# The MLP norm's sums spread by a product with a matrix of ones

## The chip, the cores and the metric

The kernel runs on one core of a Trainium2 chip. The time is the device time of one execution in microseconds (us), and the number that counts is the median over several executions. Three executions of the kernel before took 1001.45, 1001.76 and 1002.26 us.

A core has five engines that run side by side, each with its own queue of instructions worked off in order: PE (TensorE, matrix products; PEld are its loads of the stationary operand), DVE (VectorE, elementwise), ACT (ScalarE, elementwise with a function), POOL (GpSimd) and SP (SyncE, which here only issues transfers). Products land in PSUM, in banks of 128 partitions by 512 fp32 numbers. DVE and ACT read PSUM and SBUF.

## The reference, cut to what matters

One layer of a hybrid decoder for 576 tokens (512 prompt tokens and 8 x 8 sample tokens), width 1024, hidden width of the MLP 4096. The part that matters here is the last:

```python
def rmsnorm(x, g, eps):
    xf = x.astype(jnp.float32)
    y = xf * lax.rsqrt(jnp.mean(xf * xf, axis=-1, keepdims=True) + eps)
    return (y * g.astype(jnp.float32)).astype(x.dtype)

x = x + m @ lp['w_out']
hn = rmsnorm(x, lp['g_ffn'], NORM_EPS)
x = x + jnp.square(jax.nn.relu(hn @ lp['w_up'])) @ lp['w_down']
...
y_prompt = rmsnorm(hp, g_final, NORM_EPS)
```

The MLP is quadratic in `hn`, so a factor that is the same for all features of a token can be pulled out of it: with M2 = mean(x²) + eps of a token, the MLP's result is that of the unscaled input divided by M2. The kernel uses this: it multiplies x by M2 before the down projection adds to it, and multiplies the sum by R2 = 1/M2 at the end.

## The kernel before, in words

Activations lie transposed: features on the 128 partitions (8 groups `d` of 128), the 576 tokens along the free axis, cut into two halves of 288 (`HALF = ((0, 288), (288, 288))`). A per-token factor such as M2 must therefore stand in every partition: `M2` and `R2` are tiles of 128 x 576 whose rows are all alike.

Every weight matrix arrives as fp32 and is split into a high and a low part of a shorter format (ACT writes the high part, DVE the rest), and each product is made of three: high·high, high·low, low·high. One such product of 128 x 128 with 288 columns is the unit of PE's work.

The stages of the end: output projection (tiles `ps_wo`), which writes x into `ya` (lines 1128 to 1167) and adds up the squares of x over the eight feature groups into `acc` (128 x 576: what is left is a sum over the 128 partitions); then the up projection in 16 pairs (`up_pair`, line 1180), each of seven block products of twelve matmuls by a Strassen-like scheme (PSUM tiles `ua`, `ub`, `uc`, `ud`, `ux`), whose results are squared and split into `q`; then the down projection (`down`, line 1266; PSUM tile `ps_dn`), whose results are added to `ya`. The loop at line 1280 runs eight chunks `ch` of two pairs; from chunk 1 on each pair is followed by four of the eight groups of the chunk before's down projection. The down projection of the last chunks (line 1304 on) multiplies by R2 and makes the final norm.

The norm of the MLP stands inside this loop, behind the first pair (lines 1283 to 1298). `colsum` (line 234) sums `acc` over the partitions with five products, each with 128 tokens of `acc` as the stationary operand and a column of ones as the moving one; the sums come out with tokens on the partitions, in a PSUM tile of 128 x 5. DVE makes the mean plus eps (`m2`, 128 x 5) and its reciprocal (`r2`). `spread` (line 245) brings each back into 128 equal rows: five transposes on PE of a column broadcast along the free axis, each into a PSUM bank of its own (`pb_M2`, `pb_R2`), each copied to SBUF by ACT. In the profile the numbers at the ends of names are left out, so the tiles appear as `pst`, `m`, `r`, `pb_M`, `pb_R`, `M`, `R`. Two other tiles of such names (of earlier norms) share rows with `pst` and `R`.

The order of the work on each engine is made ahead of time by a planner. It takes, among the instructions whose inputs and buffers it counts as ready, the one with the lowest priority number. `prio(...)` sets that number: `FEED + 1000 * job` (negative) for loads, splits and evictions that belong to product number `job`, `FILL + 1000 * job` (positive) for the matmuls themselves. `ring["job"]` counts the products. A small offset on it puts an instruction behind or ahead of others of the same job. The planner may take an instruction long before its place in the program, if it is ready. `bank(...)` takes one of three PSUM banks in rotation; the up pair's `ux` (line 1239) is from the same three. The multiplication of `ya` by `M2` has line 1273, in `down` for the chunk 0; in the profile it has the helper's line, L61.

Of the kernel before, what the change touches and what calls it, by code (L numbers as in the profile page):

```python
# [8 lines left out]
F32 = mybir.dt.float32  # L9
# [6 lines left out]
P = 128  # L16
D = 1024
# [11 lines left out]
HALF = ((0, 288), (288, 288))  # L29
# [12 lines left out]
def tile_hybrid_step(ctx, tc, xT, xsT, ktab, vtab, s0T, ptab, w_in, vecs, w2a2, g2, lamv,  # L42
# [3 lines left out]
    PE, VE, AE, GE = nc.tensor, nc.vector, nc.scalar, nc.gpsimd  # L46
    PS = bass.MemoryType.PSUM

    def pool(name, bufs=1, stack=ctx, **kw):
        return stack.enter_context(tc.tile_pool(name=name, bufs=bufs, **kw))  # L50
# [4 lines left out]
    ring = {"job": 0}  # L55

    def act(out, in_, func=AF.Copy, **kw):
        ring["act"] = AE.activation(out=out, in_=in_, func=func, **kw)  # L58
# [9 lines left out]
    def ts(out, a, s1, op0, s2=None, op1=ALU.bypass, eng=None):  # L68
        (eng or VE).tensor_scalar(out=out, in0=a, scalar1=s1, scalar2=s2, op0=op0, op1=op1)

    def mm(out, lhsT, rhs, start=True, stop=True):
        ring["mm"] = PE.matmul(out=out, lhsT=lhsT, rhs=rhs, start=start, stop=stop)  # L72
        return ring["mm"]

    def tr(out, in_, idn):
        ring["mm"] = PE.transpose(out=out, in_=in_, identity=idn)

    def bc(ap, shape):
        return ap.broadcast_to(shape)
# [3 lines left out]
    FEED, LATE, FILL = -1000000, 500000, 1000000  # L83

    @contextmanager
    def prio(at):
        was, tc.cur_priority = tc.cur_priority, at
        yield
        tc.cur_priority = was

    MUL, ADD, SUB, MAX = ALU.mult, ALU.add, ALU.subtract, ALU.max
# [7 lines left out]
    stat = pool("stat", 2)  # L99

    def bank(name):
        return psw.tile([P, 512], F32, tag="w", name=name)

    def tbank(name):
        return psc.tile([P, 512], F32, tag="t", name=name)
# [10 lines left out]
    ones1 = const.tile([P, 1], F32, name="ones1")  # L116
# [8 lines left out]
    onesP = const.tile([P, P], F32, name="onesP")  # L125
# [108 lines left out]
    def colsum(out, src, sel, n):  # L234

        for t in range(5):
            m = min(P, NT - t * P)
            mm(out[:m, t * n:(t + 1) * n], src[:, t * P:t * P + m], sel)
# [6 lines left out]
    def spread(dst, r, name):  # L245

        for t in range(5):
            m = min(P, NT - t * P)
            pb = bank(f"pb_{name}_{t}")
            tr(pb[:, :m], bc(r[:m, t:t + 1], [m, P]), ident[:m, :m])  # L250
            act(dst[:, t * P:t * P + m], pb[:, :m])
# [19 lines left out]
    with tc.tile_pool(name="xin", bufs=2, reuse_waits="tile") as xin:  # L271
        xt = [xin.tile([P, NT], F32, name=f"x{k}", bufs=1) for k in range(KT)]
        xs_ = xin.tile([P, KT, NB], F32, name="xs", bufs=1)
        acc = xin.tile([P, NT], F32, name="acc", bufs=1)
# [3 lines left out]
        for k in range(0, KT, 4):  # L278
            for j in range(3):
                with prio(FEED + 1000 + 10 * k + j):  # L280
                    name = f"raw_{'qkv'[j]}0_{k}"
# [26 lines left out]
        pst = tbank("pst1")  # L308
# [356 lines left out]
    for h in range(HB):  # L665
        if h:
            qkv(h)
        for cc in range(2):
            GE.tensor_copy(
                out=qbd[64 * cc:64 * cc + 64, :, h, 8 * cc:8 * cc + 8],  # L670
                in_=qT[64 * cc:64 * cc + 64, h, NPR:].rearrange("p (b q) -> p b q", b=NB))
# [445 lines left out]
    R2 = fp.tile([P, NT], F32, name="R2")  # L1117
    M2 = fp.tile([P, NT], F32, name="M2")
    acc = fp.tile([P, NT], F32, name="acc2")
# [146 lines left out]
    def down(c, ds):  # L1266

        q, half = divmod(c, 2)
        his, los = ([qs[4 * c + k][:, i] for k in range(4)] for i in range(2))
        for d in ds:  # L1270
            if c == 0:
                with prio(FEED + 1000 * ring["job"] + 150):
                    tt(ya[:, d], ya[:, d], M2, MUL)

            def ev(ps, t0, n, d=d):
                o = ya[:, d, t0:t0 + n]
                tt(o, o, ps, ADD)
            dense(w_down[q, d][:, 4 * half:4 * half + 4], 4, his, los, HALF, ev, f"dn{c}{d}")

    for ch in range(8):  # L1280
        for i in range(2):
            up_pair(4 * ch + 2 * i)
            if ch == 0 and i == 0:
                with prio(FILL + 1000 * ring["job"] + 999):

                    pst = bank("pst2")
                    colsum(pst, acc, ones1, 1)
                with prio(FEED + 1000 * ring["job"]):
                    m2 = stat.tile([P, 5], F32, tag="r", name="m2")
                    r2 = stat.tile([P, 5], F32, tag="s", name="r2")  # L1290
                    VE.memset(m2, 1.0)
                    ts(m2[:, 0:4], pst[:, 0:4], 1.0 / D, MUL, 1e-6, ADD)
                    ts(m2[:64, 4:5], pst[:64, 4:5], 1.0 / D, MUL, 1e-6, ADD)
                    VE.reciprocal(out=r2, in_=m2)
                with prio(FILL + 1000 * ring["job"] + 1999):
                    spread(M2, m2, "M2")
                with prio(FILL + 1000 * ring["job"] + 9999):
                    spread(R2, r2, "R2")
            if 0 < ch < 7:
                down(ch - 1, range(4 * i, 4 * i + 4))  # L1300

# [13 lines left out]
    for t0, n in LAST:  # L1315
# [41 lines left out]
        for i, src in enumerate([acc[:, span]] + last):  # L1357
            pst = bank(f"pst3{t0}{i}")
# [20 lines left out]
        for d in range(KT):  # L1379
# [4 lines left out]
            if d + 1 in ends:  # L1384
                i = ends.index(d + 1)
# [119 lines left out]
```

## Time and profile before

| what | value |
|---|---|
| median of three runs | 1001.76 us |
| profiled execution: span from first to last instruction | 1004.0 us |
| instructions | 24422 |
| PE busy | 975.5 us (97%) |
| DVE busy | 689.5 us (69%) |
| ACT busy | 497.3 us (50%) |
| POOL busy | 88.3 us (9%) |

The page gives the profiled execution no other time than its span. It is 2.2 us above the median of the three runs. Busy times overlap between engines; the share of an engine is an average over stages that differ. "Who waited" rows give the instruction that waits, then the one that released it. The chain of waits lists, in order of time, the work that the end of the program hangs on, with the pieces of one kind next to one another merged ("x12" is twelve instructions).

### The profile page before, as it was taken

The numbers are of one execution on the slowest core, as the hardware profiler recorded it, in microseconds if no ns is written. First come the engines' busy times: TensorE is split into PE (matmuls) and PEld (weight loads), VectorE is DVE, ScalarE is ACT, GpSimd is POOL, SyncE is SP. The second block draws the span as 40 slices with busy tenths as digits, with TensorE's granted clock in tenths as the row PEclk, the third lists the DMA queues.
The fourth block names the chain that finished last, engine by engine and source line by source line (L and its number), as shares of the span: only waits on it lengthen the run. The fifth ranks groups of instructions, "written<-read, shape, count | busy, mean of one in ns | idle before, by whom it ended". The sixth has DMA issues, their size and how long they took to land.

```text
span 1004.0 us, 24422 instructions
## 1 busy us (share of the span) xinstructions
PE 975.5 (97%) x10012; PEld 919.9 (92%) x10012; DVE 689.5 (69%) x1459; ACT 497.3 (50%) x1094; POOL 88.3 (9%) x171
## 2 busy tenths in 40 slices
PE   8999999899999999999999999999999999999996
PEld 8999998898887878888889999999999999999996
DVE  6698666774946669445588798966666666666744
ACT  6576555354435344443344666644444444444732
POOL 2511001301010340000300000000000000000001
PEclk9999999999989989999999999999999999999998
DMA  7312673121111225222377642222222222221402
GB/s 265 142 66 88 204 221 120 54 64 45 43 47 57 69 87 171 80 70 102 106 215 237 195 152 74 95 85 95 85 85 95 84 85 85 85 84 44 128 10 95
DMA packets 50833, 105.75 MB, mean 105 GB/s; under 512 B 6066, under 2 KB 8114, under 8 KB 50594
## 3 DMA queue, kind: packets, MB, share of 16 engines
q1 hardware_dynamic: 47442, 96.95, 30.2%
q0 software_dynamic: 1648, 5.35, 1.4%
q8 instruction: 79, 1.29, 0.5%
q10 hardware_dynamic: 1632, 1.89, 0.5%
q14 instruction: 32, 0.26, 0.1%
HBM read 89.38 MB, written 14.78 MB: 104 GB/s over the span
## 4 chain that ended last, share of the span: by engine, by line
PE 86%; DVE 6%; ACT 3%; DMA 2%; issue 2%; POOL 1%; SPq 0%; DVEq 0%; POOLq 0%; ACTq 0%
PE ps_dn L72 21%; PE ps_g L72 9%; PE ps_z L72 8%; PE ua L1224 5%; PE ux L1224 5%; PE ps_wo L72 4%; PE uc L1224 3%; PE ud L1224 3%; PE ub L1224 3%; PE ps_k L72 2%; PE ps_brb L72 2%; PE pch L72 2%; PE ps_q L72 2%; PE ps_v L72 2%; PE pA L72 2%
## 5 line engine op out<-in xcount | busy, mean ns | idle before, releaser
L72 PE MATMUL ps_dn<-q,hi_dn 128*128 128x288 f32 x768 | 154.7, 296 | 0.0
L72 PEld LDWEIGHTS ps_dn<-q,hi_dn 128*128 128x128 f32 x768 | 122.8, 188 | 1.5
L72 PE MATMUL ps_dn<-q,lo_dn 128*128 128x288 f32 x384 | 113.2, 295 | 0.0
L72 PE MATMUL ps_g<-xl,hi_g 128*128 128x288 f32 x256 | 80.2, 313 | 0.0
L72 PE MATMUL ps_g<-xh,lo_g 128*128 128x288 f32 x256 | 79.3, 310 | 0.0
L72 PE MATMUL ps_g<-xh,hi_g 128*128 128x288 f32 x256 | 79.2, 310 | 0.0
L72 PEld LDWEIGHTS ps_dn<-q,lo_dn 128*128 128x128 f32 x384 | 72.1, 188 | 0.0
L72 PE MATMUL ps_z<-xh,lo_z 128*128 128x288 f32 (+1 forms) x224 | 69.6, 311 | 0.0
L72 PE MATMUL ps_z<-xh,hi_z 128*128 128x288 f32 (+1 forms) x224 | 68.3, 305 | 0.0
L72 PE MATMUL ps_z<-xl,hi_z 128*128 128x288 f32 (+1 forms) x224 | 67.6, 302 | 0.0
L61 DVE TENSOR_TENSOR ya<-ya,ps_dn 128x288 f32<-128x288 f32 x96 | 43.4, 453 | 29.3 <-PE ps_dn L72 29.3
L58 ACT ACTIVATE hi_dn<-raw_dn 128x512 fp32r<-128x512 f32 x48 | 30.1, 628 | 57.0 <-PE ps_dn L72 57.0
L1224 PE MATMUL ua<-h_b,hi 128*128 128x288 f32 x256 | 53.2, 298 | 0.0
L1224 PE MATMUL ux<-h_t,hi 128*128 128x288 f32 x256 | 52.3, 296 | 0.0
L58 ACT ACTIVATE c<-c 128x288 f32<-128x288 f32 x112 | 48.4, 439 | 7.5 <-DVE c L61 5.8
L72 PEld LDWEIGHTS ps_g<-xh,hi_g 128*128 128x128 f32 x256 | 49.0, 191 | 2.9 <-issue 1.6
L72 PEld LDWEIGHTS ps_g<-xl,hi_g 128*128 128x128 f32 x256 | 49.0, 191 | 1.9
L72 PEld LDWEIGHTS ps_g<-xh,lo_g 128*128 128x128 f32 x256 | 49.1, 192 | 1.4
L58 ACT ACTIVATE hi<-a 128x1024 fp32r<-128x1024 f32 (+1 forms) x32 | 27.1, 846 | 42.0 <-PE ps_dn L72 34.3
L72 PE MATMUL ps_dn<-q,w 128*128 128x320 f32 (+1 forms) x336 | 46.4, 298 | 0.0
L61 DVE TENSOR_TENSOR lo<-s,hi 128x1024 fp32r<-128x1024 f32 x32 | 39.2, 1225 | 10.2 <-ACT hi L58 10.0
L72 PEld LDWEIGHTS ps_dn<-q,w 128*128 128x128 f32 x336 | 45.3, 190 | 0.1
(395 smaller groups left out, 2801.7 us busy)
## 6 DMA issues: line engine op xcount, KB each, us to landing
a<-in_w_up_dram SPq DMA_DIRECT2D x32, 512.0 KB, 3.3
raw_dn<-in_w_down_dram SPq DMA_DIRECT2D x64, 256.0 KB, 2.9
raw_g<-in_w_in_dram SPq DMA_DIRECT2D x32, 256.0 KB, 3.2
raw_z<-in_w_in_dram SPq DMA_DIRECT2D x28, 256.0 KB, 3.0
gt_d<-gg SPq DMA_DIRECT2D x16, 288.0 KB, 2.5
g<-gt_d SPq DMA_DIRECT2D x16, 288.0 KB, 3.7
kp<-in_ktab_dram SPq DMA_DIRECT2D x16, 256.0 KB, 4.0
vp<-in_vtab_dram SPq DMA_DIRECT2D x16, 256.0 KB, 3.7
```

The source lines that it names most:

```text
L58: ring["act"] = AE.activation(out=out, in_=in_, func=func, **kw)
L61: ins = (eng or VE).tensor_tensor(out=out, in0=a, in1=b, op=op)
L72: ring["mm"] = PE.matmul(out=out, lhsT=lhsT, rhs=rhs, start=start, stop=stop)
L1224: ring["mm"] = PE.matmul(out=ps[:, :288], lhsT=l[:, k], rhs=hb[blk][:, h, k], start=start and i == 0, stop=i == 11, skip_group_check=skip)
```

## The change

The five products with a column of ones, the two small tiles and the ten transposes with their ten copies are gone. In their place, for each half of 288 tokens, one product with `onesP`, a 128 x 128 matrix of ones that the kernel already has, as the stationary operand and `acc` as the moving one: every row of the result holds the sums of all partitions. DVE makes the mean plus eps straight from PSUM into `M2`. The reciprocal is now taken by DVE of the spread tile, 128 x 288 at a time, in instructions that stand behind the first pair of chunk 2 in the program and have the priority of that place. No transfer is added, removed or moved.

```diff
             if ch == 0 and i == 0:
-                with prio(FILL + 1000 * ring["job"] + 999):
-
-                    pst = bank("pst2")
-                    colsum(pst, acc, ones1, 1)
-                with prio(FEED + 1000 * ring["job"]):
-                    m2 = stat.tile([P, 5], F32, tag="r", name="m2")
-                    r2 = stat.tile([P, 5], F32, tag="s", name="r2")
-                    VE.memset(m2, 1.0)
-                    ts(m2[:, 0:4], pst[:, 0:4], 1.0 / D, MUL, 1e-6, ADD)
-                    ts(m2[:64, 4:5], pst[:64, 4:5], 1.0 / D, MUL, 1e-6, ADD)
-                    VE.reciprocal(out=r2, in_=m2)
-                with prio(FILL + 1000 * ring["job"] + 1999):
-                    spread(M2, m2, "M2")
-                with prio(FILL + 1000 * ring["job"] + 9999):
-                    spread(R2, r2, "R2")
+                for t0, n in HALF:
+                    with prio(FILL + 1000 * ring["job"] + 999):
+                        pm2 = bank(f"pm2{t0}")
+                        mm(pm2[:, :n], onesP, acc[:, t0:t0 + n])
+                    with prio(FEED + 1000 * ring["job"]):
+                        ts(M2[:, t0:t0 + n], pm2[:, :n], 1.0 / D, MUL, 1e-6, ADD)
+            if ch == 2 and i == 0:
+                for t0, n in HALF:
+                    with prio(FEED + 1000 * ring["job"] + 900):
+                        VE.reciprocal(out=R2[:, t0:t0 + n], in_=M2[:, t0:t0 + n])
             if 0 < ch < 7:
                 down(ch - 1, range(4 * i, 4 * i + 4))
```

## The prediction

> **What bounds the kernel now.** I read the page's engine totals first, then the table of busy times by stretch around the norm, then the chain of waits in the same place, then the rows of the tiles that come and go. The totals of the page:
>
> ```profile
> span 1004.0 us, 24422 instructions
> PE 975.5 (97%) x10012; PEld 919.9 (92%) x10012; DVE 689.5 (69%) x1459; ACT 497.3 (50%) x1094; POOL 88.3 (9%) x171
> ```
>
> PE is the bound on average. Whether it is so at the norm is read from the stretches from 615 to 700 us (columns: PE, PEld, DVE, ACT, POOL busy, each with its count, then the granted clock, the DMA share and GB/s):
>
> ```profile
> 615.50:618.50 3.00, 3.00 (x25) 2.84 (x24) 2.50 (x8) 2.03 (x6) 0.00 (x0) 1.00 0.11 41
> 618.50:621.00 2.50, 2.50 (x20) 2.27 (x19) 1.72 (x5) 1.89 (x8) 0.00 (x0) 1.00 0.34 90
> 621.00:628.80 7.80, 7.80 (x61) 7.80 (x60) 7.80 (x12) 3.72 (x6) 0.00 (x0) 1.00 0.32 112
> 628.80:630.60 1.80, 1.80 (x13) 1.46 (x12) 1.80 (x4) 1.34 (x6) 0.00 (x0) 1.00 0.29 116
> 630.60:640.00 9.40, 9.40 (x73) 9.40 (x72) 8.55 (x18) 7.41 (x16) 0.00 (x0) 1.00 0.11 30
> 640.00:650.00 10.00, 10.00 (x76) 9.94 (x76) 9.76 (x19) 6.11 (x14) 0.00 (x0) 1.00 0.32 105
> 650.00:660.00 10.00, 10.00 (x78) 10.00 (x77) 4.95 (x11) 2.74 (x4) 0.00 (x0) 1.00 0.33 107
> 690.00:700.00 10.00, 10.00 (x76) 9.87 (x75) 8.85 (x19) 4.29 (x9) 0.00 (x0) 1.00 0.33 105
> ```
>
> Two things are to be seen. PE never rests, so an instruction less on PE should end the kernel earlier by its time. But DVE is as full as PE from 621 to 630.6 and nearly so to 650; it has air again only from 650 on. ACT has room everywhere. So PE's time is the gain, and DVE's is the danger.
>
> **What is removed from PE.** The chain of waits between 614 and 631 us shows the fifteen small products among the up projection's, whose blocks of twelve take 1.60 us when nothing is between them:
>
> ```profile
> 614.05 1.79 PE ux L1224 x12
> 615.83 0.12 PE pst L72 x2
> ...
> 617.46 1.25 PE uc L1224 x8
> 618.71 0.11 PE pb_M L76
> ...
> 621.13 1.59 PE ub L1224 x12
> ...
> 627.53 1.60 PE ua L1224 x12
> 629.13 0.33 PE pb_R L76 x3
> 629.45 0.26 PE ps_dn L72 x2
> 629.71 0.31 PE ua L1224
> 630.02 0.31 PE pb_R L76 x2
> 630.33 0.33 PE ua L1224
> 630.66 1.59 PE ux L1224 x12
> ```
>
> From 615.83 to 621.13 are 5.30 us, in which two whole blocks run (twelve `uc`, twelve `ua`): 2 x 1.60 = 3.20. The rest, 2.10 us, is what the column sums and the five transposes of M2 cost, with the slower matmuls that follow each of them. From 629.13 to 630.66 are 1.53 us with four ordinary matmuls, 4 x 1.60/12 = 0.53; the transposes of R2 cost 1.00 us. Together 3.10 us. The first row, 1.79 in place of 1.60, is a wait of 0.19 us for DVE that is not the norm's; I count it as staying.
>
> **What is added to PE.** Two fp32 products with a 128 x 128 stationary tile and 288 columns. The kernel has this form in `pg` (eight products; the profile shows two records for each):
>
> ```profile
> L72 PE MATMUL pg<-P,wg x16: 404/406/502, 444.4 to 518.4; 128*128 128x288 f32 x16
> 449.19 0.58 PE pg L72 x2
> 511.73 0.97 PE pg L72 x4
> 517.77 1.05 PE pg L72 x4
> ```
>
> Four records, so two products, take 0.97 to 1.05 us in the chain when they stand together, 2 x 0.58 = 1.16 when they stand apart. I take 1.05. `acc` is complete before (PE asks for it only behind the first pair), and `onesP` exists from the start, so no new wait stands in front of them. Sum on PE: -3.10 + 1.05 = -2.05 us, bounds -2.13 and -1.94.
>
> **VectorE.** The rows (mean ns stands after the busy us):
>
> ```profile
> L69 DVE TENSOR_SCALAR m<-pst 128x4 f32<-128x4 f32 x1 | 0.2, 162 | 0.5 <-PE pst L72 0.5
> L69 DVE TENSOR_SCALAR m<-pst 64x1 f32<-64x1 f32 x1 | 0.1, 140 | 0.0
> L1294 DVE RECIPROCAL r<-m 128x5 f32<-128x5 f32 x1 | 0.2, 176 | 0.0
> L69 DVE TENSOR_SCALAR r<-s 128x5 f32<-128x5 f32 x1 | 0.2, 174 | 0.0
> L558 DVE RECIPROCAL rz<-z 128x2 f32<-128x2 f32 x16 | 2.6, 161 | 4.2 <-ACT sc L58 4.0
> L69 DVE TENSOR_SCALAR ot<-po,rz 128x128 f32<-128x128 f32 x16 | 5.6, 349 | 1.0 <-PE po L72 0.8
> L61 DVE TENSOR_TENSOR ya<-ya,ps_dn 128x288 f32<-128x288 f32 x96 | 43.4, 453 | 29.3 <-PE ps_dn L72 29.3
> L1291 DVE MEMSET m<- x1: 62/62/62, 28.1 to 28.1; 128x5 f32 x1
> ```
>
> Removed: 0.16 + 0.14 + 0.18 = 0.48 us near 617.5. (The memset ran at 28.1 us, 590 us ahead of its stage, where it cost the norm nothing; this also shows how far ahead the planner takes what is ready.) Added at the same place: two means of 128 x 288 out of PSUM. The nearest rows are the 128 x 128 of the same operation (0.35, a bound from below) and the 128 x 288 addition out of PSUM (0.45); I take 0.45 each, 0.90 in all. Net 0.42 us there. The first waits for the first product, the second for the second; behind them in DVE's queue are the evictions of `ux`, which then come about 0.2 us later, and the `ux` bank is not wanted again until 630.66. The eight multiplications of `ya` by M2 (8 x 0.75 us by the row below) no longer wait for ACT, whose last copy ended at 620.74; M2 should be whole by 618.
>
> The two reciprocals of 128 x 288 have no row of their size. From two to five elements a reciprocal grows by 15 ns (161 to 176), 5 ns for one element; taken to 288 that is 0.18 + 283 x 0.005 = 1.6 us, an upper bound. From below, 0.35 as above. The scale-and-add of five elements takes 174 ns, the same as the reciprocal's 176, so I let it go like any other elementwise operation of this size: 0.45 each, 0.90 in all. [...]
>
> Where they will run matters more. Their priority is that of chunk 2, which by the chain runs near 690 us; DVE is there busy 8.85 of 10 us. But they need only M2, and the memset row shows that the planner does not wait for a program's place. I expect them in the first hole that the plan has on DVE after M2, that is somewhere between 618 and 655 us. There 0.90 us falls into the fullest stretch. It is hidden if PE has other work in hand: from 640 on the down projection of chunk 0 stands ready (its first group at 629.45 in the chain above), and from 650 to 660 DVE idles 5 us, so the lag is made good there. I cost the reciprocals, and the 0.42 us, at nothing; without that cover they would cost 1.3 us.
>
> **ScalarE, banks, transfers.** Ten copies leave ACT:
>
> ```profile
> L58 ACT ACTIVATE M<-pb_M x5: 241/278/285, 618.9 to 620.5; 128x128 f32<-128x128 f32 x4, 128x64 f32<-128x64 f32 x1
> L58 ACT ACTIVATE R<-pb_R x10: 223/277/298, 32.0 to 630.4; 128x128 f32<-128x128 f32 x8, 128x64 f32<-128x64 f32 x2
> L61 DVE TENSOR_TENSOR ya<-ya,M x8: 749/752/755, 620.9 to 630.8; 128x576 f32<-128x576 f32 x8
> ```
>
> That is 10 x 0.28 = 2.8 us less on an engine that doesn't set the pace (half of the `R` row is another norm's): nothing on the end. Eleven turns of the three shared PSUM banks become two, which can only make `ux` easier to place. R2 is first used at the last chunk's evictions, 300 us on. No transfer moves, so SP's and POOL's queues stay as they are, except that loads may be issued up to 2 us earlier as PE frees their buffers.
>
> **Sum.** -2.05 us on the profiled execution, 1004.0 to 1001.95. The runs' median is 2.2 us lower than the profiled span, and the same 2.05 us of the same stage is taken from it: 1001.76 - 2.05 = 999.7 us.
>
> **The rivals.**
>
> *Part of the gain is lost to DVE.* The planner puts the reciprocals before a split (`lo`) that PE needs at once, so PE waits for the 0.90 us: 999.7 + 0.9 = 1000.6. For it: DVE's 7.80 of 7.80 us, and the 0.19 us wait already there. Against it: PE has down products to run meanwhile.
>
> *DVE becomes the bound of the whole stretch (the slower side).* If from 618 to 650 the end follows DVE and not PE, PE's 2.05 us are worth nothing and DVE's 0.42 + 0.90 = 1.3 us are paid: 1003.1. It decides from the point where DVE's lag no longer fits between the planner's reserve of down products and the hole at 650. For it: 9.76 of 10 us before 650. Against it: PE is just as full, and no wait of PE for DVE over 0.2 us stands in this stretch.
>
> *The reciprocal is slow.* At the 1.6 us of the bound, two are 3.2 us; with 0.42 and paid in full against PE's gain, 1001.76 - 2.05 + 3.6 = 1003.3; hidden beyond 650, it costs nothing. For it: only the 5 ns an element. Against it: the equal scale-and-add. [...]
>
> *It doesn't do what it says.* The reciprocals aren't later but right behind M2; that is what I expect already, and by itself it gives the forecast or the first rival.
>
> **How the numbers follow.** Forecast 0.60 (998.9 to 1000.3: below, all of 3.10 us removed with the 0.97 for the added products and the small waits nearby gone too, with what three runs scatter; above, the added products apart and a few tenths lost), the first rival 0.20 (1000.3 to 1001.7), DVE as the bound 0.12, the slow reciprocal 0.08. From no change, a measurement of this kernel can tell about 0.2%, 2.0 us: faster means below 999.76, slower above 1003.76. The forecast lies right at that edge, so some seven tenths of its 0.60 count as faster (0.43); of the two slower rivals, which lie at 1003.1 and 1003.3 with their losses as bounded, four tenths may pass the upper edge (0.08); the rest, 0.49, is no change. The range 998.9 to 1003.2 leaves out the best of the forecast and the far end of the slow rivals, under 2 in 10.
>
> **What would show it.** The product of `pm` with four records and about 1.0 us of the chain between the first pair and the next; no `pb_M`, `pb_R`; blocks of twelve still at 1.60 us up to 660; no PE wait for DVE over 0.2 us from 615 to 660; reciprocals of some 0.45 us between 618 and 655 us. It is wrong if the new products make following blocks longer, if a reciprocal takes over 1 us, if PE shows new waits for `lo`, `c` or `ya`, or if the stages outside 605 to 660 us change their length.

## The result and the profile after

The changed kernel takes 998.84 us (median of 22 runs, 996.45 to 1001.55); the kernel before, measured beside it, 1000.97 us (22 runs, 998.76 to 1003.59). The ratio is 0.9983 with a 95% interval of 0.9975 to 0.9991: 1.7 us faster, between 0.9 and 2.5 (the bare medians are 2.1 us apart). Two later comparisons of the same pair gave 0.9986 (0.9977 to 0.9996) and 0.9976 (0.9963 to 0.9989). One execution of the kernel before in the last of them, 1520.05 us at a granted clock of 0.557, is left out of its ratio.

The totals on the page of the changed kernel:

```profile
span 999.4 us, 24380 instructions
PE 971.7 (97%) x9996; PEld 917.9 (92%) x9996; DVE 692.6 (69%) x1459; ACT 496.0 (50%) x1084; POOL 88.5 (9%) x171
```

The span is 4.6 us shorter than before's 1004.0, over twice what the runs say. The chain of waits tells where. First come rows of before's chain that were not shown: two long transfers ahead of the norm, the long run of the output projection behind them, the first product of the up projection, and the first row of the last down projection.

```profile
533.73 4.83 DMA g<-gt_d
...
555.58 7.19 DMA a<-in_w_up_dram
...
567.92 36.20 PE ps_wo L72 x271
...
604.38 1.60 PE uc L1224 x12
...
941.50 31.09 PE ps_dn L72 x216
```

And the chain of the changed kernel from its only transfer in the same place (500 to 600 us) to the last down projection:

```profile
552.38 3.52 DMA xr<-in_xT_dram
...
565.34 36.48 PE ps_wo L72 x273
601.82 1.60 PE uc L1224 x12
...
611.49 1.79 PE ux L1224 x12
613.27 0.97 PE pm L72 x4
614.24 1.59 PE uc L1224 x12
615.83 1.60 PE ua L1224 x12
617.43 1.60 PE ub L1224 x12
...
623.83 1.79 PE ux L1224 x12
...
936.91 31.03 PE ps_dn L72 x216
```

From the first `uc` to the last down projection ("the stretch" from here on) are 941.50 - 604.38 = 337.12 us before and 936.91 - 601.82 = 335.09 us after: 2.03 us shorter. From there to the end both take 62.5 us. The other 2.56 us of the profiled difference lie ahead of 604 us, where PE works off the same instructions in the same order in both; the chain of before hung there on transfers of 4.83 and 7.19 us, that of the changed kernel on one of 3.52 us, and the difference is there already when the output projection's run starts (567.92 against 565.34). In the profiles of this study the first `uc` starts anywhere from 597.3 to 604.4 us. Three profiles of the changed kernel have spans of 999.4, 997.4 and 997.0 us, and their first `uc` starts at 601.82, 599.99 and 599.46: what differs between them lies ahead of the stretch. That the scatter of the runs without a profile, some 5 us, has the same source is likely and not shown. So the stretch is the sharper measure of this change, though that of before rests on one profile. The comparisons list a time beside each span, which the page of before did not: it is about 2 us above the span. By that the profiled execution of before took some 1006 us, longer than any of the 22 runs. The profiled execution of the changed kernel, 1001.45 us, is at the slow end of its runs too.

In the stretch: `pst`, `pb_M` and `pb_R` are gone, four records of `pm` in 0.97 us stand in their place, and the blocks of twelve behind them are at 1.60 us. One small wait is new: the second pair's `ux` at 623.83 takes 1.79 us where the same block took 1.62 us before. By the timeline it starts right behind DVE's reading of that bank, `c<-ux,w`, which runs from 623.26 to 623.71 us; that it waits for it is read from this order alone.

The busy times by stretch (PE, PEld, DVE, ACT, POOL, granted clock, DMA share, GB/s):

```profile
614.30:620.60 6.30, 6.30 (x49) 6.30 (x48) 6.04 (x13) 3.55 (x8) 0.00 (x0) 1.00 0.35 119
620.60:637.00 16.40, 16.40 (x124) 16.20 (x123) 16.14 (x27) 12.68 (x25) 0.00 (x0) 1.00 0.26 83
637.00:649.60 12.60, 12.60 (x98) 12.60 (x97) 12.45 (x24) 4.80 (x12) 0.00 (x0) 1.00 0.33 103
649.60:660.80 11.20, 11.20 (x87) 11.20 (x86) 8.45 (x12) 6.41 (x12) 0.00 (x0) 1.00 0.22 70
```

PE has no idle time; DVE is at 96 to 99% up to 649.6 us. What DVE does there, by the tile view of `M` and `pm` (min/median/max in ns, first and last start):

```profile
L72 PE MATMUL pm<-acc,onesP x4: 406/406/407, 613.1 to 613.8; 128*128 128x288 f32 x4
L69 DVE TENSOR_SCALAR M<-pm x2: 447/450/452, 614.4 to 614.7; 128x288 f32<-128x288 f32 x2
L61 DVE TENSOR_TENSOR ya<-ya,M x8: 746/748/751, 617.0 to 642.5; 128x576 f32<-128x576 f32 x8
L1293 DVE RECIPROCAL R<-M x2: 1947/1948/1948, 648.6 to 651.3; 128x288 f32<-128x288 f32 x2
```

The means take the 0.45 us of the prediction. A reciprocal takes 1.95 us, over four times the 0.45 us it was given. Nothing was seen to wait for it. The timeline of DVE shows the two at the end of the down projection of chunk 0:

```profile
648.21 0.45 DVE L61 TENSOR_TENSOR ya<-ya,ps_dn 128x288 f32<-128x288 f32 x1
648.58 1.95 DVE L1293 RECIPROCAL R<-M 128x288 f32<-128x288 f32 x1
650.44 0.40 DVE L61 TENSOR_TENSOR ya<-ya,ps_dn 128x288 f32<-128x288 f32 x1
650.75 0.68 DVE L61 TENSOR_TENSOR lo_dn<-raw_dn,hi_dn 128x512 fp32r<-128x512 f32 x1
651.35 1.95 DVE L1293 RECIPROCAL R<-M 128x288 f32<-128x288 f32 x1
654.51 0.46 DVE L61 TENSOR_TENSOR u<-ub,p 128x288 f32<-128x288 f32 x1 [1.22 <-PE ub L1224]
```

Even after the second one DVE has 1.22 us with nothing to do.

### The profile page after: what moved, and what is told of

Read it like the earlier page. It is cut to its first block, busy times and chain, and to the rows that moved or that the text cites. A ratio compares the mean times of both kernels' runs of the same rounds, so it can differ in the third digit from the quotient of the medians.

```text
span 999.4 us, 24380 instructions
## 1 busy us (share of the span) xinstructions
PE 971.7 (97%) x9996; PEld 917.9 (92%) x9996; DVE 692.6 (69%) x1459; ACT 496.0 (50%) x1084; POOL 88.5 (9%) x171
## 4 chain that ended last, share of the span: by engine, by line
PE 86%; DVE 6%; ACT 3%; issue 2%; DMA 1%; POOL 1%; SPq 0%; DVEq 0%; ACTq 0%; POOLq 0%
PE ps_dn L72 21%; PE ps_g L72 9%; PE ps_z L72 8%; PE ux L1224 5%; PE ua L1224 5%; PE ps_wo L72 4%; PE ps_k L72 3%; PE ub L1224 3%; PE ud L1224 3%; PE uc L1224 3%; PE ps_brb L72 2%; PE ps_bra L72 2%; PE ps_q L72 2%; PE pch L72 2%; PE ps_v L72 2%
```

## The experiments

Theory A: PE alone sets the stretch, each product counts by its place in the chain, and VectorE's added work is hidden. Theory B: VectorE is full between 614 and 650 us, so that it counts too, and the late place of the reciprocals is what hides them. The table has the stretch of each profile and the time's ratio to the kernel before on the same chip; the text behind it tells them one by one. The experiments ran on three chips, the first four, the next four and the last four rows each on one. In three profiles the changed kernel's stretch differs by 0.1 us.

| kernel | first `uc`, us | last down projection, us | stretch, us | ratio to before, 95% |
|---|---|---|---|---|
| before | 604.38 | 941.50 | 337.12 | |
| changed | 601.82 | 936.91 | 335.09 | 0.9983 (0.9975 to 0.9991) |
| reciprocals at once | 599.48 | 934.31 | 334.83 | 0.9966 (0.9953 to 0.9978) |
| only R2 new | 601.40 | 937.44 | 336.04 | 0.9989 (0.9977 to 1.0002) |
| only M2 new | 600.15 | 937.18 | 337.03 | 0.9996 (0.9985 to 1.0006) |
| six late reciprocals | 599.46 | 934.35 | 334.89 | 0.9986 (0.9974 to 0.9997) |
| no R2 | 597.31 | 932.37 | 335.06 | 0.9985 (0.9973 to 0.9997) |
| six reciprocals at once | 597.69 | 939.95 | 342.26 | 1.0056 (1.0041 to 1.0072) |
| reciprocals of six sizes, one run | 601.34 | 936.18 | 334.84 | |
| changed, again | 599.99 | 935.02 | 335.03 | 0.9986 (0.9977 to 0.9996) |
| reciprocals at once, again | 597.29 | 932.17 | 334.88 | 0.9974 (0.9962 to 0.9985) |
| changed, beside it | 599.46 | 934.59 | 335.13 | 0.9976 (0.9963 to 0.9989) |
| no R2, again | 600.14 | 935.26 | 335.12 | 0.9974 (0.9961 to 0.9987) |
| four reciprocals at once | 600.97 | 937.80 | 336.83 | 0.9994 (0.9980 to 1.0008) |

**The reciprocals at once.**

```diff
                     with prio(FEED + 1000 * ring["job"]):
                         ts(M2[:, t0:t0 + n], pm2[:, :n], 1.0 / D, MUL, 1e-6, ADD)
-            if ch == 2 and i == 0:
                 for t0, n in HALF:
-                    with prio(FEED + 1000 * ring["job"] + 900):
+                    with prio(FEED + 1000 * ring["job"]):
                         VE.reciprocal(out=R2[:, t0:t0 + n], in_=M2[:, t0:t0 + n])
```

> The changed kernel with the two reciprocals of 128x288 put right behind the two means, ahead of everything else in VectorE's queue there, in place of the late place (where the plan set them at 648.6 us, 1.95 us each). Measured by the stretch from the first uc product to the run of 216 down products, which is 337.1 us before and 335.1 us after the change. Theory A (PE alone sets the stretch, VectorE's lag always fits under the down products): 335.1 us again, time as the changed kernel, 2 us under before. Theory B (VectorE has no reserve between 614 and 637 us; the late place is what hides the reciprocals): PE waits for splits or evictions, the stretch is 1.5 to 3.9 us longer than the changed kernel's, 336.6 to 339.0, and the time lies between 0.5 us under and 2 us over before. I expect B.

The stretch is 334.83 us, as short as the changed kernel's. I had expected B, and B is wrong for this amount. The timeline of DVE in this kernel, and the chain of waits in the same place:

```profile
613.11 3.75 DVE L1292 RECIPROCAL R<-M 128x288 f32<-128x288 f32 x2
616.78 0.39 DVE L61 TENSOR_TENSOR c<-ux,u 128x288 f32<-128x288 f32 x1
```

```profile
618.29 1.60 PE ux L1224 x12
619.89 1.60 PE ud L1224 x12
621.49 1.20 PE uc L1224 x9
622.69 1.60 PE ux L1224 x12
624.29 0.40 PE uc L1224 x3
```

DVE does nothing else from 613.11 to 616.78, and no block on PE behind the new products is longer than 1.60 us; the small wait of the second pair's `ux` is gone too. The plan puts nine matmuls of the next pair's `uc` ahead of a `ux`: the order on PE was made anew around the reciprocals.

**The two halves of the change.** First only R2 is new; the column sums and the spreading of M2 are the old lines. (The diffs from here on are against the changed kernel; `...` stands for lines left out.)

```diff
-                for t0, n in HALF:
-                    ...
-                        mm(pm2[:, :n], onesP, acc[:, t0:t0 + n])
-                    ...
+                    pst = bank("pst2")
+                    colsum(pst, acc, ones1, 1)
+                    ...
+                with prio(FILL + 1000 * ring["job"] + 1999):
+                    spread(M2, m2, "M2")
```

> Half of the change: column sums and the five transposes of M2 as before, only R2 is new (two late reciprocals, no transposes of R2). Theory A (every product removed from PE counts by its place in the chain): the stretch is 1.00 us shorter than before's 337.1, so 336.1; time about 1 us under before. A rival, that the change's gain comes from the column sums and M2 alone (R2's transposes filled a hole that PE had anyway while it waited for VectorE at 629 us): 337.1, no gain.

336.04 us, 1.08 us less than before, as theory A has it: the transposes of R2 cost their 1.00 us and filled no hole. (The ratio, 0.9989 with 0.9977 to 1.0002, can't tell this from nothing; the stretch can.) The other half keeps the product for M2, and beside it the column sums, the small reciprocal and the spreading of R2:

```diff
                         ts(M2[:, t0:t0 + n], pm2[:, :n], 1.0 / D, MUL, 1e-6, ADD)
+                    colsum(pst, acc, ones1, 1)
+                    ...
+                    VE.reciprocal(out=r2, in_=m2)
+                    spread(R2, r2, "R2")
-            if ch == 2 and i == 0:
-                ...
```

> The other half: M2 by the product with ones, but the column sums stay too, for the small reciprocal and the five transposes of R2; only the five transposes of M2 are gone from PE, and two products are added. Theory A: +1.05 for the products, -0.84 for the transposes of M2 (2.10 less 1.27 for the sums): the stretch 337.3, time within 0.5 us of before. A rival, that most of the gain is M2 being ready earlier (618 in place of 621 us) and ScalarE being free: 335.5 to 336.3, 1 us or more under before.

337.03 us, 0.09 less than before where theory A had 0.2 more. So M2's earlier time and ScalarE's lighter load bring 0.3 us at most, not the 1 us or more of the rival. The two halves together are 1.17 of the 2.03 us. The other 0.86 us comes with the column sums, which drop out only when neither M2 nor R2 needs them; no run takes them out alone. In the chain of this kernel they still stand, with 0.99 us in one piece:

```profile
613.49 0.99 PE pst L72 x10
```

**Where VectorE's cover ends.** Three times the late reciprocals, then three times and twice the reciprocals at once (the repeats write the same values again). In the late place:

```diff
-                for t0, n in HALF:
-                    ...
+                for j in range(3):
+                    for t0, n in HALF:
+                        ...
```

> The changed kernel with the two late reciprocals taken three times over (six of 1.95 us, 11.7 us of VectorE; the extra four only repeat the result). It measures how much of VectorE's idle time at that place covers. Theory A (VectorE has 2.8 us idle from 649.6 to 660.8 and 5.4 us from 673 to 684, after two reciprocals): 7.8 us more fit, stretch 335.1 to 335.4. Theory B (a block of 1.95 us holds up an eviction of the down projection, whose banks turn every 1.6 us): 0.3 to 0.5 us for each that stands among down products, stretch 336.3 to 337.1.

334.89 us: six late reciprocals, 11.5 us of DVE by the timeline between 646 and 670 us, leave the stretch as it is. The part behind it is about half a microsecond longer than in the changed kernel (its span of 997.3 less 934.35 is 62.95 us, against 62.5). By the chain that lies over 250 us behind the reciprocals, in two pieces: the first row of the last down projection has 31.27 us in place of 31.03, the last two transposes `pb` 0.70 in place of 0.45. Why these are longer is not shown.

Then the reciprocals at once, repeated (`HALF * 3`, and `HALF * 2` further on):

```diff
-            if ch == 2 and i == 0:
-                for t0, n in HALF:
-                    with prio(FEED + 1000 * ring["job"] + 900):
+                for t0, n in HALF * 3:
+                    with prio(FEED + 1000 * ring["job"]):
                         VE.reciprocal(out=R2[:, t0:t0 + n], in_=M2[:, t0:t0 + n])
```

> The two reciprocals right behind the means, taken three times over: 11.7 us of VectorE at 613 us, where 3.9 us cost nothing. It asks where VectorE's lag is no longer hidden. Theory A (the plan always finds PE other work): stretch from the first uc product to the 216 down products 334.8 to 335.4. Theory C (the reserve is finite: VectorE idles about 4.6 us between 605 and 650 us in the kernel before, and after that only the down products of chunk 0, which need VectorE's q, are left): 11.7 less 4.6, some 5 to 7 us of PE waiting, stretch 340 to 342, the time 3 to 5 us over before. I expect C.

342.26 us: this one breaks. The row of PE's waits from 600 to 660 us, the reciprocals in the timeline of DVE, and the busy times by stretch of this kernel:

```profile
PE ud L1224 <- DVE u L61: 5.3, 1, 5.3
```

```profile
611.33 10.99 DVE L1292 RECIPROCAL R<-M 128x288 f32<-128x288 f32 x6
```

```profile
618.90:621.70 2.80, 0.00 (x1) 0.00 (x0) 2.80 (x2) 0.00 (x0) 0.00 (x0) 1.00 0.00 0
621.70:628.50 6.80, 4.32 (x18) 4.32 (x19) 6.07 (x12) 2.53 (x7) 0.00 (x0) 0.50 0.00 0
```

PE stands 5.3 us before `ud`, whose bank waits for the eviction `u` behind the six reciprocals. Then it is paid a second time: the granted clock falls to 0.50 while PE still waits, 2.8 us after its last matmul, and stays there until 628.50 us (the 3.4 us of the next expectation are a part of this). PE works 4.32 us of that at half clock, and the twelve matmuls of `ud` take 3.25 us in the chain where a block elsewhere takes 1.60. By those two times, 3.25 and 1.60 us, the 4.32 us would have been about half at the full clock, so by estimate 2.2 us are lost to the clock. 5.3 + 2.2 are 7.5 us, and the stretch is 7.4 us longer than with two reciprocals. In this run the clock falls after 2.8 us of idle time and comes back after 4.3 us of work; what sets these lengths is not shown.

> Four reciprocals right behind the means, 7.8 us of VectorE, between 3.9 us (which cost nothing) and 11.7 us (PE waited 5.3 us for VectorE's u, and the clock was at 0.5 for the 3.4 us after that; stretch 342.3). If the cover is 11.7 less 5.3, 6.4 us, PE waits 1.4 us and keeps its clock: stretch 336.2 to 336.8. If the plan is what breaks (it set the products in an order for other lengths), the wait need not follow the sum, and the stretch is 335 or over 338.

336.83 us, with this wait on PE, and these four reciprocals on DVE:

```profile
PE ud L1224 <- DVE u L61: 1.7, 1, 1.7
```

```profile
614.59 7.38 DVE L1292 RECIPROCAL R<-M 128x288 f32<-128x288 f32 x4
```

The clock stayed at 1.00 here. The cover is the time of the reciprocals less the wait. The timeline gives that time as 7.38 and 10.99 us, less than four and six times 1.95, because the rows of neighbours overlap a little (in the changed kernel's timeline the first, of 1.95 us from 648.58, ends at 650.53, and the next row starts at 650.44). By this run the cover is 7.38 - 1.7 = 5.7 us, by the one with six 10.99 - 5.3 = 5.7 us. The two agree, so in these runs the wait follows the sum, and the plan is not what breaks. At this place, where DVE looks full, some 5.7 us of extra work at one stroke fit in front of PE's first wait for it.

**The price of a reciprocal.**

```diff
-                for t0, n in HALF:
+                for t0, n in ((0, 32), (32, 32), (64, 64), (128, 128), (256, 256), (0, 576)):
```

> The price of the reciprocal by its size: in the late place six reciprocals with 32, 32, 64, 128, 256 and 576 elements on each partition (together R2 is written twice). Theory A (a fixed part and 6.26 ns an element, the line through 176 ns at 5 and 1948 ns at 288): 345, 345, 545, 946, 1748 and 3751 ns. A rival, that small ones run at one element per 1.04 ns and large ones fall into a slower form: 200 to 230 ns at 32 and 64.

The groups by form (busy us, mean ns):

```profile
L1293 DVE RECIPROCAL R<-M 128x576 f32<-128x576 f32 x1 | 3.8, 3752 | 0.0
L1293 DVE RECIPROCAL R<-M 128x256 f32<-128x256 f32 x1 | 1.7, 1696 | 0.0
L1293 DVE RECIPROCAL R<-M 128x128 f32<-128x128 f32 x1 | 0.9, 895 | 0.0
L1293 DVE RECIPROCAL R<-M 128x32 f32<-128x32 f32 x2 | 0.7, 347 | 0.0
L1293 DVE RECIPROCAL R<-M 128x64 f32<-128x64 f32 x1 | 0.5, 494 | 0.0
```

347, 494, 895, 1696 and 3752 ns against 345, 545, 946, 1748 and 3751 of theory A: a line of 6.26 ns an element (from 128 to 256: 801 ns for 128), with the middle three some 50 ns below it. The rival's 1.04 ns an element is what elementwise rows of before show (453 ns at 288 elements, 752 at 576: 299 ns for 288); 347 ns at 32 and 494 at 64 are far from its 200 to 230, so none of these sizes has shown a faster form. This kernel's six reciprocals together put some 7.5 us into the late place, and its stretch, 334.84 us, is again the changed kernel's.

**A version without R2, and the comparison of the three that are fastest.** The final norm divides by a root mean square, so a factor common to all features of a token falls out of it, but for the epsilon. ScalarE writes the epsilon, times the square of M2, into `acc`, and the final squares are added to it:

```diff
-                        VE.reciprocal(out=R2[:, t0:t0 + n], in_=M2[:, t0:t0 + n])
+                    act(acc, M2, AF.Square, scale=math.sqrt(1e-6 * D / P))
...
-                tt(r, ps, o, ADD)
-                tt(o, r, R2[:, span], MUL)
+                tt(o, ps, o, ADD)
```

> No reciprocal at all. The final norm divides by the root mean square, so the factor R2 falls out of it if the epsilon is multiplied by the square of M2: ScalarE writes eps*D/128*M2*M2 into acc (one instruction of 128x576), the final squares are added to that, and the 16 multiplications of the last evictions by R2 go. PE keeps the changed kernel's products. Measured from the first uc product to the end of the span, which is 399.6 us before and 397.6 us in the changed kernel. Theory A (PE and the tail's chain alone count): the stretch to the 216 down products 335.1 as in the changed kernel, the tail 0.39 us shorter, since one multiplication by R2 stands in it: 397.2. A rival, that the multiplications also hold up the last down products' evictions: 396.5 or less. Time 2 to 3 us under before.

The stretch is the changed kernel's (335.06). Behind it, the tail's chain has `ya` alone where it had `fin`, `s` and `ya`, 0.43 us in place of 0.89. The changed kernel, and this one:

```profile
989.57 0.42 DVE fin L61
989.99 0.08 DVE s L69
990.07 0.39 DVE ya L61
```

```profile
985.02 0.43 DVE ya L61
```

From the last down projection to the end are 994.3 - 932.37 = 61.93 us against 62.49, 62.38 and 62.41 in three profiles of the changed kernel: half a microsecond, which the times can't tell from nothing. With the two repeats on one chip:

> The kernel with the reciprocals right behind the means once more, on one chip with the changed kernel. Its first ratio to before was 0.9966, the changed kernel's 0.9983 and 0.9986, but its stretch from the first uc product to the 216 down products was only 0.2 us shorter (334.8 against 335.1 and 335.0). Theory A (the ratio's surplus is the scatter of transfers ahead of the norm): ratio 0.998, the same as the changed kernel's beside it within 0.001, stretch 334.8. A rival, that the early place really gains another 1.5 us: the ratio 0.0015 below the changed kernel's again.

> The changed kernel unaltered, as the other side of that comparison: stretch 335.1, ratio to before 0.9983 to 0.9986.

> The kernel without R2 once more. From its first profile: the stretch as in the changed kernel (335.06), from there to the end 61.93 in place of 62.4 to 62.5. Theory A: the same again, ratio 0.0005 below the changed kernel's beside it, which the timing can't resolve.

0.9974, 0.9976 and 0.9974: the surplus of the first run with the reciprocals at once (0.9966) did not come back, and the measurement can't tell the three apart. The stretches again differ by 0.2 us (334.88 with the reciprocals at once, 335.13 and 335.12) and the tail without R2 is again 61.94 us (997.2 - 935.26). The changed kernel unaltered had been expected, and was found, in its first repeat:

> The changed kernel unaltered, beside the others on one chip. Every theory expects the stretch of 335.1 us again, within 0.2 us, and about 2 us under before.

## Why the prediction was right, and where it was not

*What bounds.* Right. PE is busy without a gap before and after (337.12 of the stretch's 337.12 us, 335.09 of 335.09), and every kernel whose extra work on DVE stays within the cover follows the count of PE's products to 0.3 us.

*What is removed and added on PE.* Right to a tenth. 3.10 us removed; `pm` took 0.97, the lowest of the rows used, not 1.05; the new wait at `ux` costs 0.17, which the sum did not have. That is 3.10 - 0.97 - 0.17 = 1.96, and the stretch shows 2.03, with 2.09 and 1.99 in the repeats (2.05 predicted). The transposes of R2 alone gave 1.08 where the prediction had 1.00, so that part was right too. The new product without dropping the column sums is no gain (0.09).

*The means.* Right: 0.45 us each.

*The reciprocals' price.* Wrong, and this is the step that failed. The prediction let a reciprocal go "like any other elementwise operation" at 0.45 us, because five elements cost the same as in a scale-and-add. It is 1.95 us. Even what was called an upper bound, 1.6 us, was none: it came from a difference of 15 ns between two rows (161 and 176), where the sixteen instructions of the first alone spread from 151 to 166 ns, and 3 x 6.26 = 19 ns was the truth. Five elements cannot show a slope against a fixed part of some 145 ns (176 less 5 x 6.26). At 1.95 us the slow-reciprocal rival was true in its cause, and wrong in its effect: 3.9 us of DVE cost nothing. By the prediction's own sign, a reciprocal of over 1 us, this step was wrong. That the time came out all the same is luck in this term: the prediction had no size for the cover, and counted on hiding 1.3 us of added work where over 4 us had to be hidden.

*Where they run, and what hides them.* Right in the main: not in chunk 2 but where the plan first had room on DVE, at 648.6 us, inside the 618 to 655 given. That the planner reached ahead decided nothing, since the same work right behind the means costs nothing either. The prediction named the down products as the cover; the runs put a size to it, about 5.7 us behind the means. With the reciprocals there, the cover is the up projection's own blocks, which the plan rearranges: the chain of that run has no down product before 634 us. The full DVE column did not mean that DVE was the pace.

*The rivals.* DVE as the bound fell with the runs that put two reciprocals behind the means and lost nothing. It becomes true above some 5.7 us; with six reciprocals it then cost more than the excess, 7.4 us for a wait of 5.3, because the clock dropped to 0.50. Part of the gain lost to DVE: 0.17 us of it, in a new wait that follows `c`, not 0.9 and not for `lo`.

*The number.* The size forecast, 2.05 us, lies inside the interval of 0.9 to 2.5 us, and the stretch agrees with it to a few hundredths. The forecast time, 999.7 us, was taken from a base of 1001.76 us, the median of three executions. From that base the ratio gives 1000.06 us. Beside the changed kernel the base was 1000.97 us, which is why the bare median, 998.84, lies 0.9 us under the forecast and just under the 998.9 of its range. The profiled spans differ by 4.6 us, and the prediction made no allowance for that: it took the 2.2 us between before's span and its median as given, when that execution was a slow one by its transfers ahead of the norm. So the stages ahead of 605 us did change their length, which the prediction had named as a sign of being wrong; as the order of work there is the same, the change isn't the cause.

## What to carry to other kernels

When one engine has no gap in a stretch, count the instructions that leave it and join it by their place in the chain, slower neighbours included; here fifteen small products cost as much as 23 large matmuls (3.10 us at 0.133 us each). A second engine that is 98% busy in the same stretch is not yet a bound (3.9 us more of DVE's work cost nothing here): ask how long PE can go on before it needs that engine's next result, and measure that by adding work. Don't take an operation's price from rows so small that the fixed part hides the slope (161 and 176 ns at two and five elements, 1948 at 288), and compare two profiles over a stretch that holds the change and nothing else.

## What the runs showed of the hardware

VectorE's reciprocal took 6.26 ns for each element on a partition (895 ns at 128 and 1696 at 256; 1948 at 288 and 3752 at 576) over a fixed part of some 145 ns, by estimate from the 176 ns at five elements, and about four times an addition from PSUM of the same shape (1948 against 450 ns at 288). With six reciprocals at once, in a wait of 5.3 us on TensorE, the granted clock fell to 0.50 after 2.8 us and came back 4.3 us after the work did; with four, a wait of 1.7 us left it at 1.00.
